# A hybrid decoder layer on one core: paired query loads, merged key and bias loads, six weight splits on VectorE, half of the lead-in fill moved ahead of the value compression

## The chip, the core and the metric

The kernel runs on one core of a Trainium2 chip. The metric is the device time of one launch in microseconds; less is better. The core has a matrix engine (TensorE, PE in the profile; its loads of the stationary operand are shown as PEld), VectorE (DVE), ScalarE (ACT), GpSimd (POOL) and SyncE (SP), which issues all DMAs here.

## The reference

One layer over 1,024 tokens of width 1,024 in float32, cut to what matters:

```python
h = rms_norm(x, attn_norm)
a_conv, q, kc_r, vc_r, ks, vs, kw, vw, g = split(h @ w_in)   # one wide projection
conv_out = swish(layer_norm(causal_depthwise_conv31(u * sigmoid(v))))   # 256 channels
kc, vc = compress(kc_r, ...), compress(vc_r, ...)   # blocks of 32, stride 16: silu(x @ w1) @ w2
# 12 query heads in 4 groups; each group has one key/value head per branch
s_c = softmax(q kc - slope * distance)              # compressed branch; also picks blocks
top = top_k(block_sums(s_c) + forced, 8)            # 8 of 16 blocks of 64 tokens
s_s = softmax(q ks[top] - slope * distance)         # selected branch
s_w = softmax(q kw - slope * distance), last 512 tokens   # window branch
out = g0 * (s_c @ vc) + g1 * (s_s @ vs[top]) + g2 * (s_w @ vw)
x = x + concat(conv_out, out) @ w_out
x = x + (silu(h2 @ w_gate) * (h2 @ w_up)) @ w_down  # h2 = rms_norm(x), hidden width 2816
return rms_norm(x, final_norm)
```

## The kernel before

Every float32 product is three matmuls on a high and a low part: a tile is cast to its high part on ACT, and the low part is the difference, by DVE for activations (`split`) and by POOL for weights (`load_w`: one DMA into one of two `raw` buffers, one ACT cast, and four POOL subtractions of 128x256; three buffers each for high and low part). With `eng` set to another engine, `load_w` makes one subtraction over the whole chunk instead; only the two chunks of the first value projection (`head`) do so before.

The kernel is traced in one order, and a planner places each engine's instructions from that order with simulated times. On the chip every engine then runs its own list strictly in order, and a wait at the head of a list holds all that is behind it. SP's list holds all the DMAs. The kernel has eight PSUM banks in four tags: `s` (2), `t` (3), `o` (1), `z` (2). `turn[1]` names the tags from which `acc_bank` takes the next projection's bank.

The lead-in works on the first 512 tokens (half 0). The `Drive` runs a main line of matmuls, each yielding an estimate of its duration, and steps side jobs when their time has come:

- four conv chunks (`conv_in`, L519), then the two chunks of the key compression's input (`compress_in`, L431), which writes `xh` and `xl` by ACT casts and DVE subtractions; beside it the 62 depthwise taps of half 0 on DVE (`conv_taps`, L537) and POOL's tables (`tables`);
- the window values (`values`, L307, matmuls `vo`);
- the key compression (`compress`, L453: 96 matmuls `h` in four weight chunks), and after each chunk one query projection (`project_d`, L415: 24 matmuls `zo`), in turn by `in_turn`;
- more projections, the value compression's input and the value compression in the same manner, with the stages of the compressed branch (`cmp_stage`, L597) and the tail of the convolution (`conv_tail`, L561) as side jobs. `conv_tail` makes, for each of four token tiles, a transposition `cl`, layer norm on DVE and POOL into `cn`, and after `CONV_LAG` of the drive's time a transposition `cm` of `cn`;
- `compress_v` (L495), which copies the hidden rows to `dup` on DVE and makes the matmuls `vc` from them; then the pools of the lead-in are closed, and the attention's pool `pc` takes their space.

After that 48 matmuls of the fill (`fill_all`: the projections of tokens 512 to 1,023, then output projection and feed-forward) run by themselves, and the rest of the fill is woven into `attention` (L678). Part 0 of the attention has 4 groups of 4 token tiles, part 1 the 4 later tiles of each group. For each tile it does the window branch (br 1) and the selected branch (br 0). `load` (L687), called by the tile's first `scores`, loads keys (in four DMAs) and values once per group, and the tile's queries (in two DMAs, in part 1 a third and three of the bias); queries have two buffers, keys and values one per branch. When the attention is done the second half of the tokens goes through the output projection, and then the feed-forward fills the time to the end.

Of the kernel before, what the change touches and what calls it, by code (L numbers as in the profile page):

```python
# [19 lines left out]
P = 128  # L20
# [59 lines left out]
ACCS2 = "tzz"  # L80
ACCS3 = "z"
PACE_C = 0
CONV_LAG = 5.0
STAGE_GAPS = 5.0, 0.7, 10.0, 0.0
PIECES = 4

# [2 lines left out]
def tile_hymba(ctx: ExitStack, tc, x, attn_norm, w_in, conv_w, conv_b, conv_ln_g, conv_ln_b,  # L89
# [183 lines left out]
    hhi = [quarters(h, 0) for h in range(2)]  # L273
    hlo = [quarters(h, 1) for h in range(2)]

    def win_chunk(c0):
        return load_w([(0, w_in[0, :, c0:c0 + P])], KT, P)


    def value_loads(c0, g0, eng=pool):  # L280
        return [lambda kh=kh: load_w([(0, w_in[0, kh * 512:(kh + 1) * 512, c0:c0 + 256]),
                                      (256, w_in[0, kh * 512:(kh + 1) * 512, C_G + g0:C_G + g0 + 18])], 4, 274, eng)
                for kh in range(2)]
# [30 lines left out]
    for t in range(6):  # L314
        if t < 4:
            if t % 2 == 0:
                x2 = pa.tile([P, 2, DM], F32, tag="xc", name="xt", bufs=2)
            xts.append(x2[:, t % 2, :])
        else:
            xts.append(p2.tile([P, DM], F32, tag="xt", name="xt", bufs=2))  # L320
        sp.dma_start(xts[t], x[0, t * P:(t + 1) * P, :])
        if t == 0:
            grow = a4("grow")
            sp.dma_start(grow, attn_norm[0].partition_broadcast(P))
        if t in (1, 2):
            head.append(value_loads(C_VS, 0, dve)[t - 1]())
        if t == 5:
            first = Feed([lambda c=c: win_chunk(c) for ct in range(2) for c in (CONV + ct * P, ct * P)])
            first.ahead(2)
    for t in range(4):  # L330
        norm_rows(xts[t], xts[t], grow, pa, a4("junk"))
# [346 lines left out]
    def attention(p, bufs, extra, ratio):  # L678
# [8 lines left out]
        def load(st):  # L687
            part, g, i, br = st
            hf = i // 4
            ns = parts[part][-1] + 1  # L690
            if i == parts[part][0]:
                assert not hf or (("kv", g // 2) in done and ("v", g // 2) in done)
                src = (ks_d, kw_d)[br]
                kk = p.tile([P, 2, T], F32R, tag=f"k{br}", name="kt", bufs=bufs["k"])[:, :, :ns * P]
                kf = kk.bitcast(F32)
                sl = src[:, g * 64:(g + 1) * 64, :ns * P]
                sp.dma_start(kf[0:64, 0, :], sl[0])
                sp.dma_start(kf[64:128, 0, :], sl[0])
                sp.dma_start(kf[0:64, 1, :], sl[1])
                if br == 1 or not hf:  # L700
                    sp.dma_start(kf[64:128, 1, :], sl[1])
                else:
                    sp.dma_start(kf[64:80, 1, :], hot_d)
                kt[part, g, br] = kk
                vv = p.tile([P, NT, P], F32R, tag=f"v{br}", name="vt", bufs=bufs["v"])[:, :ns, :]
                sp.dma_start(vv.bitcast(F32), (vs_d, vw_d)[br][:ns * P, g, :].rearrange("(k p) d -> p k d", p=P))
                vt[part, g, br] = vv
            if br == 1:
                cols_i = slice(i * P, (i + 1) * P)
                q2 = p.tile([P, 2, REP, P], F32R, tag="q", name="q2", bufs=bufs["q"])  # L710
                qf = q2.bitcast(F32)
                qs = [q_d[w, g * 192:(g + 1) * 192, cols_i].rearrange("(r d) t -> d r t", d=HD) for w in range(2)]
                sp.dma_start(qf[0:64, 0], qs[0])
                sp.dma_start(qf[64:128, 0], qs[1])
                if hf:
                    sp.dma_start(qf[0:64, 1], qs[0])
                    assert ("bias", g) in done
                    il = i - 4
                    for r in range(REP):
                        sp.dma_start(qf[64:80, 1, r, :], bias_d[g, :, il * P:(il + 1) * P])  # L720
                q2s[g, i] = q2

        def load_pct(st):
            part, g, i, br = st
# [5 lines left out]
        def scores(st, r):  # L730
            part, g, i, br = st
            hf = i // 4
            if r == 0:
                load(st)
            nk = size(st)
            k0 = i + 1 - nk
# [3 lines left out]
            if r == 0:  # L740
                prs[st] = [p.tile([P, REP], F32, tag="l3", name="l3", bufs=26)]
            l3 = prs[st][0]
            q2, kk_ = q2s[g, i], kt[part, g, br]
            if hf:
                pr = p.tile([P, T], F32, tag="pr", name="pr", bufs=bufs["pr"])
            else:
# [5 lines left out]
            for a, e in zip(edges, edges[1:]):  # L752
                s = bank("s", "s")
                sv = s[:, :e - a]
                kk = slice(k0 * P + a, k0 * P + e)
                pe.matmul(sv, q2[:, 0, r, :], kk_[:, 0, kk], start=True, stop=False)  # L756
                if br == 0 and hf:
                    pe.matmul(sv, q2[0:80, 1, r, :], kk_[0:80, 1, kk], start=False, stop=True)  # L758
                else:
                    pe.matmul(sv, q2[:, 0, r, :], kk_[:, 1, kk], start=False, stop=True)  # L760
                dur += 2 * max(0.107, (e - a) / 2400.0)
                mn = p.tile([P, 1], F32, tag="m", name="m", bufs=16)
                t0 = T if br and nk == 5 and a == 0 else T - n + a
                dve.tensor_tensor_reduce(pr[:, a:e], sv, base[:, t0:t0 + e - a], SLOPES[g * REP + r], m,  # L764
                                         ALU.add, ALU.min, mn)
                m = mn
# [59 lines left out]
        for n in range(-1, len(steps)):  # L826
# [7 lines left out]
            asked = max(asked, want)  # L834
            if n < 0:
                load_pct(steps[0])
            elif steps[n][3] and n + 2 < len(steps):
                load_pct(steps[n + 2])
            ts = range(size(steps[n])) if n >= 0 else []
# [41 lines left out]
            yield n  # L881


    def in_turn(main, others, part):
        others = iter(others)
        for n, d in enumerate(main):
            yield d
            if n % part == part - 1:
                yield from next(others, ())
        for o in others:  # L890
            yield from o
# [5 lines left out]
    def mixed_in(a, b):  # L897
        return [ld for pair in itertools.zip_longest(a, b) for ld in pair if ld]

    kvl = kv_loads()  # L900
    first.loads += ([lambda m=m: win_chunk(C_KC + m * P) for m in range(2)] + value_loads(C_VW, 18)
                    + mixed_in(w1_loads(cmp_k_w1), [q_load(m) for m in range(4)]) + [q_load(4), q_load(5)]
                    + [lambda m=m: win_chunk(C_VC + m * P) for m in range(2)] + kvl[:1]
                    + mixed_in(w1_loads(cmp_v_w1), kvl[1:3]) + kvl[3:])
    drive = Drive()
# [6 lines left out]
    drive.run(compress_in(first, 68, xk))  # L912
    drive.run(values(first, 18, vw_d, 0))
    drive.run(in_turn(compress(*xk, first, cmp_k_w2, "s", kk),
                      [project_d(first, q_d, m * P, (0,), True) for m in range(4)], 24))
    turn[1] = ACCS2
    drive.run(project_d(first, q_d, 4 * P, (0,), True))
    compress_k(*kk)
# [9 lines left out]
                      [project_d(first, dst, r, (0,)) for dst, r in ((ks_d, 0), (kw_d, P))], 24))  # L928
    drive.side(stages_in(3))
    drive.run(project_d(first, ks_d, P, (0,)))  # L930
    compress_v(*kv)
    p2_stack.close()
    pa_stack.close()

    pc_stack, pc = open_pool("pc", "right")
    turn[1] = "z"

    def fill_b():
        f1 = Feed([q_load(0), q_load(1)] + value_loads(C_VS, 0) + [q_load(2)] + value_loads(C_VW, 18)
                  + [q_load(m) for m in (3, 4, 5)] + kv_loads() + conv_loads())  # L940
# [267 lines left out]
        yield from conv_tail(1)  # L1208

    fill, slow = fill_all(), conv_rest()  # L1210
    with ExitStack():
        drive.run(itertools.islice(fill, FIRST_B))
        drive.rest()
        weave(attention(pc, BUFS, extra, (RATIO_B, RATIO_C)), fill, (RATIO_B, RATIO_C), slow=slow)
        run(slow)
        pc_stack.close()
        pd_stack, pd = open_pool("pd", "right")
        weave(second(pd), fill, RATIO_D, LEAD_D)
        n0 = early[0]
        early[0] = -1  # L1220
        run(fill)
# [47 lines left out]
```

## Time and profile before

| | |
|---|---|
| median of 3 runs | 1500.84 us (1500.1 to 1503.89) |
| the profiled execution | 1499.39 us |
| its span in the trace | 1497.7 us |
| PE busy | 1447.7 us, 97% |
| mean granted clock of TensorE | 0.991 of full speed |

The span runs from the first to the last instruction of the trace. Busy time is the union of an engine's instructions; matmuls overlap their neighbours, so a busy PE can still run at half of its clock. A number in brackets behind a timeline row is the idle time of that engine just before it, and behind the arrow stands what released it.

### The profile page before, as it was taken

What the parts mean: (1) busy time and instruction counts of PE and PEld (TensorE: products, weight loads), DVE (VectorE), ACT (ScalarE), POOL (GpSimd) and SP (SyncE); (2) the same over time, 40 slices, a digit from 0 to 9 for tenths busy, and PEclk for the clock granted to TensorE, in tenths of its full rate; (3) what the DMA queues carried; (4) which work ended last, traced back from release to release, by engine and by line L of the source; (5) the groups of instructions that cost most, each with busy time, mean ns of one, the idle gap of its engine ahead of it and who ended that gap; (6) DMA issues with size and microseconds to landing.
All of it is one profiled execution on the core that took longest, in us unless ns stands there. A gap on an engine that the chain in (4) does not pass through costs nothing.

```text
span 1497.7 us, 21904 instructions
## 1 busy us (share of the span) xinstructions
PE 1447.7 (97%) x7271; PEld 1214.5 (81%) x7271; DVE 818.4 (55%) x1928; ACT 730.4 (49%) x1477; POOL 839.1 (56%) x1188
## 2 busy tenths in 40 slices
PE   7999989998999999999999999999999999999997
PEld 7788878887878878888888888778788888888885
DVE  6992465778777778687577686222425222222323
ACT  6233577678765676666666655322322222222223
POOL 4666463767766546655655555644533455555554
PEclk9999999999999999999999999999999999999999
DMA  7337477667579334345335223743223323333332
GB/s 231 87 98 199 133 209 235 178 189 188 166 243 242 86 100 121 90 106 130 90 95 141 77 62 93 234 137 95 84 71 108 104 84 99 99 98 98 93 91 84
DMA packets 234222, 193.62 MB, mean 129 GB/s; under 512 B 15881, under 2 KB 204141, under 8 KB 234109
## 3 DMA queue, kind: packets, MB, share of 16 engines
q1 hardware_dynamic: 234108, 192.22, 44.2%
q8 instruction: 58, 0.95, 0.3%
q14 instruction: 56, 0.45, 0.1%
HBM read 158.42 MB, written 33.75 MB: 128 GB/s over the span
## 4 chain that ended last, share of the span: by engine, by line
PE 66%; DVE 4%; DMA 4%; ACT 2%; POOL 2%; issue 1%; SPq 0%; DVEq 0%; POOLq 0%; ACTq 0%
PE gu L1115 30%; PE dn L1135 15%; PE pt L783 4%; PE wo L1055 3%; PE s L756 2%; PE o L801 2%; PE o L800 2%; PE wo L1076 2%; PE s L760 1%; PE s L758 1%; DMA w_raw<-in_w_in_dram 1%; DMA mix<-mix_d 1%; DMA o_raw<-in_w_out_dram 1%; PE cv L145 1%; DVE pl L233 1%
## 5 line engine op out<-in xcount | busy, mean ns | idle before, releaser
L229 POOL TENSOR_TENSOR w_lo<-w_raw,w_hi 128x256 fp32r<-128x256 f32 (+1 forms) x720 | 550.9, 800 | 359.5 <-ACT w_hi L225 346.6
L1115 PE MATMUL gu<-h,w_hi 128*128 128x512 f32 x1408 | 453.4, 396 | 0.0
L225 ACT CAST w_hi<-w_raw 128x1024 fp32r<-128x1024 f32 (+1 forms) x182 | 190.0, 1049 | 364.9 <-PE gu L1115 161.6
L1115 PEld LDWEIGHTS gu<-h,w_hi 128*128 128x128 f32 x1408 | 263.4, 188 | 56.6
L1115 PE MATMUL gu<-h,w_lo 128*128 128x512 f32 x704 | 278.1, 395 | 0.0
L1135 PE MATMUL dn<-w_hi,aw 128*128 128x512 f32 x704 | 234.9, 397 | 2.4 <-DVE af L1122 1.5
L777 POOL TENSOR_SCALAR pr<-pr,l,gates 128x640 f32<-128x640 f32 (+5 forms) x192 | 151.6, 806 | 94.5 <-DVE l L772 86.3
L767 ACT ACTIVATE pr<-pr,m 128x640 f32<-128x640 f32 (+5 forms) x192 | 141.5, 738 | 84.3 <-DVE m L764 77.6
L1140 DVE TENSOR_TENSOR x<-dn,x 128x512 f32<-128x512 f32 x176 | 114.2, 684 | 106.1 <-PE dn L1135 105.5
L1122 DVE TENSOR_TENSOR af<-gu,af 128x512 f32<-128x512 f32 x44 | 30.3, 688 | 240.1 <-PE gu L1115 155.2
L1135 PEld LDWEIGHTS dn<-w_hi,aw 128*128 128x128 f32 x704 | 132.2, 188 | 33.4 <-DVE af L1122 2.2
L233 DVE TENSOR_TENSOR pl<-pt,ph 128x384 fp32r<-128x384 f32 x264 | 139.2, 550 | 36.6 <-ACT ph L233 35.3
L1115 PEld LDWEIGHTS gu<-h,w_lo 128*128 128x128 f32 x704 | 132.3, 188 | 28.6
L233 ACT CAST ph<-pt 128x384 fp32r<-128x384 f32 x264 | 117.5, 478 | 66.6 <-PE pt L783 54.4
L1135 PE MATMUL dn<-w_lo,aw 128*128 128x512 f32 x352 | 138.7, 394 | 0.0
L783 PE MATMUL pt<-ident,pr 128*128 128x128 f32 x792 | 137.0, 273 | 0.6 <-DVE pl L233 0.4
L764 DVE CUSTOM_DVE_ANT_0 pr<-s,base 128x384 f32<-128x384 f32 (+3 forms) x192 | 101.4, 533 | 24.8 <-PE s L760 14.2
L783 PEld LDWEIGHTS pt<-ident,pr 128*128 128x128 f32 x792 | 101.4, 140 | 16.3 <-POOL pr L777 1.7
L145 PE MATMUL zo<-h,w_hi 128*128 128x512 f32 x320 | 108.9, 408 | 4.0 <-ACT af L475 2.3
L756 PE MATMUL s<-kt,q 128*128 128x384 f32 (+3 forms) x288 | 100.3, 351 | 5.0 <-DMA q<-q_d 3.2
L800 PE MATMUL o<-ph,vt 128*128 128x384 f32 x264 | 98.9, 374 | 0.3 <-ACT ph L233 0.3
L801 PE MATMUL o<-pl,vt 128*128 128x384 f32 x264 | 93.2, 353 | 0.5 <-DVE pl L233 0.5
(208 smaller groups left out, 2322.0 us busy)
## 6 DMA issues: line engine op xcount, KB each, us to landing
w_raw<-in_w_gate_up_dram SPq DMA_DIRECT2D x84, 512.0 KB, 3.9
w_raw<-in_w_down_dram SPq DMA_DIRECT2D x42, 512.0 KB, 3.4
w_raw<-in_w_in_dram SPq DMA_DIRECT2D x40, 512.0 KB, 5.0
q<-q_d SPq DMA_DIRECT2D x80, 96.0 KB, 3.4
qc<-q_d SPq DMA_DIRECT2D x32, 192.0 KB, 4.1
pc_d<-pct SPq DMA_DIRECT2D x16, 384.0 KB, 3.4
pct<-pc_d SPq DMA_DIRECT2D x32, 192.0 KB, 3.1
mix_d<-oh SPq DMA_DIRECT2D x64, 96.0 KB, 3.2
```

Of the source, the lines that this page charges most:

```text
L145: lastpe[0] = pe.matmul(*args, **kw)
L225: act.copy(hi[:, :n], raw[:, :n])
L229: eng.tensor_sub(lo[:, q], raw[:, q], hi[:, q].bitcast(F32))
L233: return act.copy(hi, src), dve.tensor_sub(lo, src, hi.bitcast(F32))
L756: pe.matmul(sv, q2[:, 0, r, :], kk_[:, 0, kk], start=True, stop=False)
L767: act.activation(pr[:, :n], pr[:, :n], AF.Exp, bias=m, scale=-1.0, accum_out=l3[:, r:r + 1])
L777: pool.tensor_scalar(x_, x_, l3[:, r2:r2 + 1], gates[:, i, c:c + 1], op0=ALU.mult, op1=ALU.mult)
L783: pe.transpose(pt[:, r * P:(r + 1) * P], prs[st][1 + r][:, kk * P:(kk + 1) * P], ident)
L800: pe.matmul(o[:, :384], v, ph, start=False, stop=False)
L801: pe.matmul(o[:, :384], v, pl, start=False, stop=last)
L1115: pe.matmul(o, w[:, k, :], h2[si][h][k // 4][:, k % 4, :], start=n == 0, stop=n == 3 * KT - 1)
L1135: pe.matmul(o, aws[si][:, a, k, t * P:(t + 1) * P], b[:, 0, ch * 512:(ch + 1) * 512], start=n == 0, stop=n == 5)
```

## The change

- The four conv chunks and the two chunks of the key compression's input have their low parts made by DVE, one subtraction each, instead of four on POOL.
- The first query projection runs whole before the key compression, and the weight chunks are loaded in that order.
- In part 0 one pair of DMAs loads the queries of two token tiles. A group's keys come in two DMAs instead of four (in part 1's selected branch three instead of four). The bias of a tile comes in one DMA with a repeated source instead of three.
- The loads of the first two attention steps stand together ahead of the first scores.
- 24 of the 48 matmuls of the lead-in fill (the first query projection of half 1) stand ahead of `compress_v`, with their bank from tag `t`; the other 24 follow it.
- `CONV_LAG` is 8 instead of 5.

```diff
-CONV_LAG = 5.0
+CONV_LAG = 8.0
...
-    def win_chunk(c0):
-        return load_w([(0, w_in[0, :, c0:c0 + P])], KT, P)
+    def win_chunk(c0, eng=pool):
+        return load_w([(0, w_in[0, :, c0:c0 + P])], KT, P, eng)
...
-            first = Feed([lambda c=c: win_chunk(c) for ct in range(2) for c in (CONV + ct * P, ct * P)])
+            first = Feed([lambda c=c: win_chunk(c, dve) for ct in range(2) for c in (CONV + ct * P, ct * P)])
...
-                sl = src[:, g * 64:(g + 1) * 64, :ns * P]
-                sp.dma_start(kf[0:64, 0, :], sl[0])
-                sp.dma_start(kf[64:128, 0, :], sl[0])
-                sp.dma_start(kf[0:64, 1, :], sl[1])
+                sl = src[:, g * 64:(g + 1) * 64, :ns * P].rearrange("w d t -> d w t")
+                sp.dma_start(kf[0:64], sl)
                 if br == 1 or not hf:
-                    sp.dma_start(kf[64:128, 1, :], sl[1])
+                    sp.dma_start(kf[64:128], sl)
                 else:
+                    sp.dma_start(kf[64:128, 0, :], sl[:, 0, :])
                     sp.dma_start(kf[64:80, 1, :], hot_d)
...
-            if br == 1:
+            if br == 1 and not hf:
+                if i % 2 == 0:
+                    q2 = p.tile([P, REP, 2 * P], F32R, tag="q", name="q2", bufs=bufs["q"])
+                    for w in range(2):
+                        sp.dma_start(q2[w * 64:(w + 1) * 64].bitcast(F32),
+                                     q_d[w, g * 192:(g + 1) * 192, i * P:(i + 2) * P].rearrange("(r d) t -> d r t", d=HD))
+                    for j in range(2):
+                        q2s[g, i + j] = [[q2[:, r, j * P:(j + 1) * P]] * 2 for r in range(REP)]
+            elif br == 1:
...
-                    for r in range(REP):
-                        sp.dma_start(qf[64:80, 1, r, :], bias_d[g, :, il * P:(il + 1) * P])
+                sp.dma_start(qf[64:80, 1], bias_d[g, :, il * P:(il + 1) * P].unsqueeze(1).to_broadcast([16, REP, P]))
...
-            if r == 0:
+            if r == 0 and st not in steps[:2]:
                 load(st)
...
             if n < 0:
                 load_pct(steps[0])
+                load(steps[0])
+                load(steps[1])
...
-    def in_turn(main, others, part):
+    def in_turn(main, others, part, ahead=0):
         others = iter(others)
+        for _ in range(ahead):
+            yield from next(others)
...
-    first.loads += ([lambda m=m: win_chunk(C_KC + m * P) for m in range(2)] + value_loads(C_VW, 18)
-                    + mixed_in(w1_loads(cmp_k_w1), [q_load(m) for m in range(4)]) + [q_load(4), q_load(5)]
+    first.loads += ([lambda m=m: win_chunk(C_KC + m * P, dve) for m in range(2)] + value_loads(C_VW, 18)
+                    + mixed_in([q_load(m) for m in range(4)], w1_loads(cmp_k_w1)) + [q_load(4), q_load(5)]
...
-                      [project_d(first, q_d, m * P, (0,), True) for m in range(4)], 24))
+                      [project_d(first, q_d, m * P, (0,), True) for m in range(4)], 24, 1))
...
-    compress_v(*kv)
-    p2_stack.close()
-    pa_stack.close()
-
-    pc_stack, pc = open_pool("pc", "right")
-    turn[1] = "z"
...
     fill, slow = fill_all(), conv_rest()
+    turn[:] = -1, ACCS2
+    drive.run(itertools.islice(fill, FIRST_B // 2))
+    compress_v(*kv)
+    p2_stack.close()
+    pa_stack.close()
+
+    pc_stack, pc = open_pool("pc", "right")
     with ExitStack():
-        drive.run(itertools.islice(fill, FIRST_B))
+        drive.run(itertools.islice(fill, FIRST_B // 2))
         drive.rest()
+        turn[1] = "z"
```

## Rows read from the trace of the kernel before

**Rows 1.** The page: busy time, share of the span and instructions by engine.
```profile
PE 1447.7 (97%) x7271; PEld 1214.5 (81%) x7271; DVE 818.4 (55%) x1928; ACT 730.4 (49%) x1477; POOL 839.1 (56%) x1188
```

**Rows 2.** PE's timeline, rows with idle time: start, duration, instruction, idle before, releaser.
```profile
42.03 1.09 PE L248 MATMUL tp<-ident,xt 128*128 128x128 f32 x8 [2.29 <-DVE h L233]
...
91.18 0.68 PE L145 MATMUL h<-xh,w_hi 128*128 128x264 f32 x2 [1.74 <-ACT xh L233]
...
205.56 0.41 PE L582 MATMUL cm<-ident,cn 128*128 128x128 f32 x2 [2.67 <-DVE cl L626]
...
208.45 0.79 PE L145 MATMUL zo<-h,w_hi 128*128 128x512 f32 x1 [2.26 <-ACT af L475]
...
242.78 0.30 PE L760 MATMUL s<-kt,q 128*128 128x128 f32 x1 [1.72 <-DMA kt<-ks_d]
...
266.35 0.47 PE L756 MATMUL s<-kt,q 128*128 128x512 f32 x1 [0.81 <-DMA q<-q_d]
...
357.32 0.42 PE L756 MATMUL s<-kt,q 128*128 128x384 f32 x1 [2.39 <-DMA q<-q_d]
...
476.11 0.51 PE L1055 MATMUL wo<-w_hi,mix 128*128 128x512 f32 x1 [1.89 <-DMA mix<-mix_d]
```

**Rows 3.** Windows: length, busy of PE, PEld, DVE, ACT, POOL, clock, DMA, GB/s.
```profile
88.00:92.00 4.00, 2.26 (x16) 2.03 (x14) 3.94 (x8) 1.11 (x3) 0.00 (x0) 0.92 0.61 197
92.00:96.00 4.00, 3.57 (x21) 3.30 (x20) 3.88 (x10) 0.89 (x2) 0.00 (x0) 0.65 0.22 84
204.00:208.00 4.00, 0.63 (x4) 0.42 (x4) 3.10 (x12) 3.95 (x11) 2.34 (x4) 0.93 1.01 242
208.00:212.00 4.00, 3.55 (x8) 2.81 (x9) 3.58 (x9) 3.97 (x8) 4.00 (x6) 0.50 0.43 146
212.00:216.00 4.00, 4.00 (x14) 3.18 (x13) 0.25 (x1) 3.95 (x13) 1.67 (x3) 0.72 0.77 184
356.00:360.00 4.00, 2.68 (x10) 2.20 (x10) 1.30 (x6) 3.55 (x11) 2.42 (x5) 0.70 0.40 129
360.00:364.00 4.00, 4.00 (x21) 3.37 (x21) 3.52 (x11) 2.15 (x7) 3.71 (x8) 0.87 0.38 108
600.00:700.00 100.00, 100.00 (x548) 86.82 (x547) 71.89 (x179) 66.51 (x118) 60.33 (x82) 1.00 0.40 105
```

**Rows 4.** Splits, taps, normalisations by line: ns min/median/max, first and last start.
```profile
L229 POOL TENSOR_TENSOR w_lo<-w_raw,w_hi x720: 715/743/1979, 19.6 to 1475.3; 128x256 fp32r<-128x256 f32 x174, 128x274 fp32r<-128x274 f32 x6
L229 DVE TENSOR_TENSOR w_lo<-w_raw,w_hi x2: 1289/1290/1290, 11.6 to 14.1; 128x1096 fp32r<-128x1096 f32 x2
L553 DVE SCALAR_TENSOR_TENSOR cacc<-y,cols,cacc x62: 705/752/1409, 46.2 to 920.4; 128x512 f32<-128x512 f32 x62
...
L241 DVE SCALAR_TENSOR_TENSOR xt<-xt,rs,grow x8: 1277/1284/7315, 6.6 to 32.8; 128x1024 f32<-128x1024 f32 x8
```

**Rows 5.** Timelines of POOL around 35 us and of DVE at 46 us.
```profile
32.78 2.81 POOL L229 TENSOR_TENSOR w_lo<-w_raw,w_hi 128x256 fp32r<-128x256 f32 x4
...
36.93 3.80 POOL L229 TENSOR_TENSOR w_lo<-w_raw,w_hi 128x256 fp32r<-128x256 f32 x4
...
46.17 5.28 DVE L553 SCALAR_TENSOR_TENSOR cacc<-y,cols,cacc 128x512 f32<-128x512 f32 x5
```

**Rows 6.** Timelines at 205 to 221 us: DVE, ACT and PE.
```profile
204.88 0.54 DVE L576 TENSOR_SCALAR cn<-cl,mv,crs 128x256 f32<-128x256 f32 x1
...
219.90 0.75 DVE L501 CAST dup<-al 128x512 fp32r<-128x512 f32 x2
...
215.04 0.47 ACT L475 ACTIVATE af<-h,bc 128x256 f32<-128x256 f32 x1
...
220.61 0.19 PE L506 MATMUL vc<-w2h,dup 128*128 128x64 f32 x1
```

**Rows 7.** SP's query loads by line; one load on the chain of waits.
```profile
L713 SPq DMA_DIRECT2D q<-q_d x32: 573/598/675, 232.2 to 845.2; - x32
...
351.36 5.87 DMA q<-q_d
```

More of the change, by code (lines that the diff above doesn't have):

```diff
@@ L714, in load @@
                 sp.dma_start(qf[64:128, 0], qs[1])
[L715 to L718, printed above, removed]
-                    for r in range(REP):
-                        sp.dma_start(qf[64:80, 1, r, :], bias_d[g, :, il * P:(il + 1) * P])
-                q2s[g, i] = q2
+                sp.dma_start(qf[0:64, 1], qs[0])
+                assert ("bias", g) in done
+                il = i - 4
+                sp.dma_start(qf[64:80, 1], bias_d[g, :, il * P:(il + 1) * P].unsqueeze(1).to_broadcast([16, REP, P]))
+                q2s[g, i] = [[q2[:, w, r, :] for w in range(2)] for r in range(REP)]
         def load_pct(st):
@@ L742, in scores @@
             l3 = prs[st][0]
-            q2, kk_ = q2s[g, i], kt[part, g, br]
+            q2, kk_ = q2s[g, i][r], kt[part, g, br]
             if hf:
@@ L755, in scores @@
                 kk = slice(k0 * P + a, k0 * P + e)
-                pe.matmul(sv, q2[:, 0, r, :], kk_[:, 0, kk], start=True, stop=False)
+                pe.matmul(sv, q2[0], kk_[:, 0, kk], start=True, stop=False)
                 if br == 0 and hf:
-                    pe.matmul(sv, q2[0:80, 1, r, :], kk_[0:80, 1, kk], start=False, stop=True)
+                    pe.matmul(sv, q2[1][0:80], kk_[0:80, 1, kk], start=False, stop=True)
                 else:
-                    pe.matmul(sv, q2[:, 0, r, :], kk_[:, 1, kk], start=False, stop=True)
+                    pe.matmul(sv, q2[0], kk_[:, 1, kk], start=False, stop=True)
                 dur += 2 * max(0.107, (e - a) / 2400.0)
```

## The prediction, as it was put on record

> **What bounds the kernel now.** I read the page first, then PE's own timeline for its idle places, then windows around those, and last the other engines' timelines beside them. The page says that PE is busy for 1447.7 of 1497.7 us [rows 1], so what an edit can win is PE's idle time, about 50 us (some 15 of it at the two ends), and the time in which PE works at a lowered clock. The change takes no matmul away. PE's timeline shows where the idle time lies: before 560 us, in waits of 0.2 to 2.7 us, eight of which stand in [rows 2]. From 600 to 700 us PE is busy for the whole of the window at full clock [rows 3], and the later stages look the same; nothing done there can help. So each edit is worth what it takes from the waits in the first 360 us.
>
> A wait of two microseconds costs more than itself. After the waits at 91, 205 and 357 us the windows show a granted clock of 0.50 to 0.92, down to the lower of the two levels, 1.2 GHz, at 208 to 212 us [rows 3]. I price this as busy time times what the clock lacks of 1: (0.08 x 2.26) + (0.35 x 3.57) = 1.4 us at 88 to 96; (0.07 x 0.63) + (0.50 x 3.55) + (0.28 x 4.0) = 2.9 at 204 to 216; (0.30 x 2.68) + (0.13 x 4.0) = 1.3 at 356 to 364. The waits at 42, 242 and 266 us have no such price beside them.
>
> **The change part by part.**
>
> *DVE splits.* A chunk's split now takes four POOL instructions of 0.743 us in the median, 3.0 us; on DVE one of 1,096 columns took 1.290 us [rows 4], so 1,024 columns are estimated at 1.21 and six chunks at 7.2 us. They fall between 19 and 60 us, in front of DVE's taps, which leave it hardly any free time (it is busy for 3.94 of 4 us at 88, just before the wait for `xh` [rows 3]). Against this stands what POOL's splits cost DVE. Of eight row normalisations, 1.284 us each in the median, one took 7.315 [rows 4]; it is the last, from 32.84 to 40.16, and ended only in the second of two groups of POOL splits (32.78 and 36.93) [rows 5]. The transposition's wait of 2.29 us at 42.03 follows from it, as the subtraction that frees its bank stood behind it on DVE. The taps at 46 us took 5.28 / 5 = 1.06 us each beside POOL [rows 5], against a median of 0.752 [rows 4]. With the splits off POOL I expect 6.0 us back at the normalisation and about 0.3 on each of 12 taps, 3.6: 9.6 back for 7.2 spent, so the `xl` subtractions behind which the key compression waits end no later. The wait at 42 us goes: 2.3, less 0.5 for a split that stands ahead of a subtraction that PE needs (bounds 0 and two splits, 2.4). I take 1.8.
>
> The Trainium skill has a rule on just this (page "SBUF — State Buffer", section "Who interferes with whom"): of a DVE instruction with two SBUF inputs and a GpSimd instruction that reads SBUF, the second to start waits until the first is finished. By that rule the normalisation would lose one POOL instruction, about 0.7 us; the row shows it losing 6.0, through several of them. Here the row decides, and it makes moving the splits worth more than the rule would.
>
> *Query projection ahead.* PE waits 1.74 us at 91.18 for `xh` [rows 2], and the clock takes 1.4: 3.1 in all. With the change 24 matmuls of 128x512, which at 0.232 us each (24 follow one another in 5.6 us) take 5.6 us, stand between the values and the compression, more than the wait. The chunk order follows the order of use, so the number of loads, casts and splits is the same; each compression chunk is needed 5.6 us later and each projection chunk 3.0 earlier. At the end the last compression chunk has one projection behind it instead of two to hide the way to `kc`; the second was not needed if ACT is free then. Worth 0 to 3.1; I take 2.9.
>
> *CONV_LAG and half of the fill.* The wait of 2.67 us at 205.56 is that of `cm` for `cn`, which DVE finished only at 205.4 [rows 2, 6], and the 2.26 us at 208.45 are the projection behind it, waiting for a bank of tag `t`; with the clock 2.9, so 7.8 us. In the drive's time the second `cm` stands 5 after its `cl`, beside the last compression matmuls; with 8 it comes after the projection that follows, two or three matmuls into the first half of the fill, 5.6 us later on PE. The projection then finds `cm`, `cl` and a bank of the tag free earlier, and both waits go. But something comes back. In the profile `vc` starts at 220.61 without a wait, and that is just when the last DVE copy to `dup` is done (219.90 + 0.75); its chain stood on ACT behind the exponentials of the compressed branch, the second `af` at 215.04 [rows 6]. Without the waits PE is through the projection and the first half of the fill (11.2 us from 202.9) at 214.1, and if the planner puts `vc` right there, PE waits until `dup` is there: between 0 (the chain moves up with PE, or the second half of the fill is put ahead) and 6.5 us, and again a slow clock. The last `cm`, which with the larger lag is left to the end of the drive right behind its `cl`, may cost another 0 to 2.7, the wait of today. I take 3.4 of both, nearer to nothing, since the `cm` work leaves ACT in that stretch: 7.8 - 3.4 = 4.4. On its way the half fill also brings three weight chunks (five DMAs, three casts, twelve POOL splits) ahead of `compress_v`; its copies, subtractions and matmuls are on DVE and PE, and its one ACT cast comes last, so these pass it by. Its bank is one of three of tag `t` for 5.6 us.
>
> *Merged and paired loads.* A query load holds SP for 0.598 us [rows 7]. In part 0 the pairs save 16 of 32, the keys 16 of 32; in part 1 the bias saves 32 issues and the keys 12, off PE's path (600 to 700 us). The pair of tiles 2 and 3 goes into the buffer that the pair of the group before left, instead of waiting for tile 0's last scores of its own group. The load on the chain of waits at 351.36 took 5.87 us to its release of `s` [rows 7] at 357.32; with pairs it can be issued up to a group's tile earlier. That wait with its clock is 2.4 + 1.3 = 3.7; I take 3.3. The 0.81 at 266.35 is an odd tile's, which comes with its pair: 0.6. The 1.72 at 242.78 waits for `ks`, whose load stood behind the queries; hoisted and shorter by two issues it comes several microseconds earlier: 1.4. Each could save nothing if the larger transfer lands later by as much.
>
> *Sum.* 1.8 + 2.9 + 4.4 + 3.3 + 0.6 + 1.4 = 14.4 us. Since the planner makes the order anew, I count one new wait like that at 476.11, 1.89 us [rows 2] and 1.3 for the clock: -3. That leaves 11.4. The profiled execution, 1499.39 us, becomes 1488.0; it was 1.45 below the median, so the median becomes 1489.
>
> **The rivals.**
>
> 1. *The waits move on.* `vc` and the last `cm` get back all of it (6.5 + 2.7), and the reorder another such wait. Then 14.4 becomes 14.4 - 5.8 - 6 = 2.6: 1498, within the noise. For it speaks that `vc` has no slack today; against it, that the fill's other half and the values are independent work that may be put ahead. Chance 0.20.
>
> 2. *All of it is kept.* The six places give 2.3 + 3.1 + 7.8 + 1.7 + 0.8 + 3.7 = 19.4 us and no new wait comes: 1481. For it speaks that PE has independent work at every one of them; against it, the many in-order lists. Chance 0.12.
>
> 3. *Later landing at the group changes: slower.* A key load of one transfer twice as long has to land whole before the first scores of a group; keys have a single buffer per branch, so the load can't start earlier. If this shows as a wait like the one at 357 us, it costs 3.7 us at each of the 16 group loads. Three of them take back what I forecast; from five on (18.5) the kernel is slower by over 0.3%: 1489 + 18.5 = 1507. Against it speaks that the bytes are the same, that SP is done two issues (1.2 us) sooner, and that today only one group load shows a wait, the 1.72. Chance 0.10.
>
> **How the numbers follow.** The forecast, 1489, has 0.58. Runs of this kernel lie within 0.25% of each other, so I call 0.3%, 4.5 us, the bound of what can be told: faster means under 1496.3. The forecast and rival 2 are faster, 0.70; rival 1 is the same, 0.20; rival 3 slower, 0.10. The range runs from rival 2's time to just beyond rival 1's, 1480 to 1501, and leaves out rival 3 and little else.
>
> **What would show it.** Right: no idle above 1 us before the late transpositions near 40 us; the normalisation at 1.3 us; no wait for `xh` at the first `h`; no wait for `cn` at 200 to 210 us and a clock of 1.00 there; no wait of `s` for a query DMA near 350 us. Wrong: a wait before `vc` of over 3 us, a slow clock at 212 to 230 us, a new wait at a group's first scores, or DVE's taps that end later than now, with the first `h` waiting still.

## The result, and the profile after

The changed kernel takes 1514.7 us in the median of 4 runs (1511.62 to 1516.43), before takes 1502.37 on the same chip (1500.1 to 1504.54). The ratio is 1.008, with a 95% interval of 1.0055 to 1.0105: it is slower, by 12 us, where 1489 was forecast. The profiled execution took 1514.14 us, its span 1512.4.

PE has 7271 matmuls as before. The page's line of busy times answers to [rows 1]: POOL has lost the six chunks' splits, PE is busy 7.7 us longer and idle 7.0 us longer.

```profile
PE 1455.4 (96%) x7271; PEld 1217.2 (80%) x7271; DVE 817.8 (54%) x1934; ACT 724.8 (48%) x1473; POOL 821.5 (54%) x1164
```

PE's timeline after, rows with idle time, to be held against [rows 2]:

```profile
104.99 0.52 PE L145 MATMUL h<-xh,w_hi 128*128 128x264 f32 x2 [1.39 <-ACT w_hi L225]
106.11 0.81 PE L145 MATMUL h<-xh,w_lo 128*128 128x264 f32 x2 [0.60 <-POOL w_lo L229]
139.05 0.39 PE L491 MATMUL kc<-ah,w2h 128*128 128x256 f32 x1 [3.56 <-ACT ah L233]
206.18 0.50 PE L145 MATMUL zo<-h,w_hi 128*128 128x512 f32 x1 [0.92 <-ACT cf L585]
270.35 0.52 PE L145 MATMUL vo<-w_hi,h 128*128 128x274 f32 x2 [2.06 <-ACT w_hi L225]
352.56 0.80 PE L145 MATMUL zo<-h,w_hi 128*128 128x512 f32 x1 [2.88 <-ACT w_hi L225]
495.05 0.79 PE L1058 MATMUL wo<-w_hi,mix 128*128 128x512 f32 x1 [2.77 <-DMA mix<-mix_d]
1025.83 1.20 PE L1079 MATMUL wo<-o_hi,mix 128*128 128x512 f32 x4 [1.55 <-ACT o_hi L1005]
1058.16 2.82 PE L248 MATMUL tp<-ident,rows 128*128 128x128 f32 x12 [3.01 <-DVE rows L241]
```

The six places that the forecast named are clean: no wait at 42 and at 91, 0.92 us instead of 4.93 near 205, no `s` that waits for a load. In their stead stand the weights at 105, `kc` at 139, weights again at 270 and 352, and two waits behind 1,000 us, in stages that no edit touches. The windows of [rows 3], after, show the same: full clock and a busy PE at 88 to 96 and at 208 to 216, where before had 0.92, 0.65, 0.50 and 0.72.

```profile
88.00:92.00 4.00, 4.00 (x27) 3.69 (x26) 3.87 (x9) 1.02 (x2) 0.00 (x0) 1.00 0.64 220
92.00:96.00 4.00, 4.00 (x27) 3.61 (x26) 4.00 (x5) 3.01 (x4) 3.52 (x4) 1.00 0.18 66
204.00:208.00 4.00, 3.08 (x20) 2.64 (x19) 3.33 (x13) 3.92 (x8) 3.25 (x6) 1.00 1.00 264
208.00:212.00 4.00, 4.00 (x21) 3.20 (x19) 3.43 (x7) 2.19 (x4) 4.00 (x6) 1.00 0.84 237
212.00:216.00 4.00, 4.00 (x21) 3.02 (x18) 1.52 (x5) 3.43 (x13) 1.15 (x2) 1.00 0.48 131
356.00:360.00 4.00, 4.00 (x16) 3.31 (x15) 1.90 (x7) 2.41 (x12) 0.74 (x2) 0.70 0.27 102
```

**Where the time went.** Waits alone don't tell it, since two orders can't be compared by the clock on the wall. So I give each matmul of both traces one fixed price, the usual spacing of its shape in before, and ask when each kernel has done the same amount of this work. The table below names an amount by the time at which before had done it, and gives how much later (+) the other kernel had. (To be ahead or behind is always meant against before.) The changed kernel is 2.1 us ahead at 81 us, 2.5 behind at 181, 3.0 ahead again at 225, 6.5 behind at 384, 5.3 behind at 950, and 15.0 behind from 1,107 to the end. Three losses, then: 4.6 us around the key compression, 9.5 in the first part of the attention, 9.7 in the second output projection; and two gains, 2.1 and 5.5, which are the DVE splits and the waits at 205. The 9.5 is the least firm of them: the difference swings with each wait of either kernel, and at 480 us the changed kernel is only 1.7 behind.

The last loss is plain in the windows too. The second set's output projection and norm lie between 960 and 1,080 us; PE starts 166 + 174 + 186 = 526 matmuls there before, and 161 + 163 + 163 = 487 after. From 950 to 1,110 us PE is idle for 2.0 us before and for 7.8 after. Windows of before, then of the changed kernel:

```profile
960.00:1000.00 40.00, 38.83 (x166) 31.05 (x167) 11.31 (x18) 7.19 (x11) 18.52 (x26) 1.00 0.37 113
1000.00:1040.00 40.00, 40.00 (x174) 32.43 (x173) 7.22 (x10) 10.41 (x15) 21.90 (x31) 1.00 0.47 157
1040.00:1080.00 40.00, 39.18 (x186) 31.58 (x185) 19.73 (x30) 16.59 (x26) 20.62 (x29) 1.00 0.26 79
```
```profile
960.00:1000.00 40.00, 38.22 (x161) 29.40 (x160) 9.34 (x14) 8.73 (x12) 15.29 (x21) 1.00 0.38 112
1000.00:1040.00 40.00, 38.20 (x163) 29.88 (x162) 6.93 (x10) 8.45 (x13) 22.37 (x32) 1.00 0.45 151
1040.00:1080.00 40.00, 35.96 (x163) 28.80 (x162) 19.33 (x30) 14.43 (x24) 16.79 (x24) 0.96 0.24 73
```

One piece of it can be followed by hand. DVE's normalisation needs the row of norm weights, which SP loads in 0.58 us of issue. Before, SP issued it at 1044.21 and DVE normalised at 1047.92. After, SP's list has a weight load ahead of it, and that one waited for a buffer until POOL's split was over (1047.23 + 3.33 us); so the row was issued at 1051.02 and DVE went on at 1056.82. SP and POOL, then DVE, of the changed kernel:

```profile
1047.23 3.33 POOL L229 TENSOR_TENSOR w_lo<-w_raw,w_hi 128x256 fp32r<-128x256 f32 x4
...
1050.59 0.38 SPq L224 DMA_DIRECT2D w_raw<-in_w_gate_up_dram  x1
1051.02 0.58 SPq L1087 DMA_DIRECT2D rows<-in_ffn_norm_dram  x1
...
1056.82 3.68 DVE L241 SCALAR_TENSOR_TENSOR rows<-x,rs,rows 128x1024 f32<-128x1024 f32 x3 [4.07 <-DMA rows<-in_ffn_norm_dram]
```

The same of before, with the transpositions on PE behind it:

```profile
1044.21 0.33 SPq L1084 DMA_DIRECT2D rows<-in_ffn_norm_dram  x1
...
1047.92 1.28 DVE L241 SCALAR_TENSOR_TENSOR rows<-x,rs,rows 128x1024 f32<-128x1024 f32 x1 [1.32 <-DMA rows<-in_ffn_norm_dram]
...
1049.26 1.09 PE L248 MATMUL tp<-ident,rows 128*128 128x128 f32 x8 [0.67 <-DVE rows L241]
```

So the row explains a part only: DVE stood 4.07 us for it instead of 1.32, and PE's transpositions behind it 3.01 instead of 0.67.

Two theories follow. "Edit": the lag, the half fill and the projection ahead lose by what they do. "Order": small edits make the planner lay out the attention and all that is woven into it anew, and that order is worse than the one of before, whatever the edit was.

### The profile page after: what moved, and what is told of

It is laid out like the page before. It is cut to its first block, busy times and chain, and to the rows that moved or that the text cites. A ratio compares the mean times of both kernels' runs of the same rounds, so it can differ in the third digit from the quotient of the medians.

```text
span 1512.4 us, 21784 instructions
## 1 busy us (share of the span) xinstructions
PE 1455.4 (96%) x7271; PEld 1217.2 (80%) x7271; DVE 817.8 (54%) x1934; ACT 724.8 (48%) x1473; POOL 821.5 (54%) x1164
## 4 chain that ended last, share of the span: by engine, by line
PE 68%; DMA 10%; DVE 9%; POOL 5%; ACT 4%; issue 3%; SPq 0%; DVEq 0%; ACTq 0%; POOLq 0%
PE gu L1118 30%; PE dn L1138 15%; PE pt L789 5%; DMA w_raw<-in_w_in_dram 4%; PE zo L145 3%; POOL w_lo L229 3%; PE wo L1058 3%; PE o L807 2%; PE o L806 2%; PE s L762 2%; DMA o_raw<-in_w_out_dram 2%; DVE cacc L553 2%; PE zc L145 1%; DMA mix<-mix_d 1%; POOL o_lo L1008 1%
## 5 line engine op out<-in xcount | busy, mean ns | idle before, releaser
L229 POOL TENSOR_TENSOR w_lo<-w_raw,w_hi 128x256 fp32r<-128x256 f32 (+1 forms) x696 | 530.5, 795 | 361.5 <-ACT w_hi L225 348.7
L789 PEld LDWEIGHTS pt<-ident,pr 128*128 128x128 f32 x792 | 102.8, 141 | 18.7 <-POOL pr L783 1.9
```

The source lines that it names most:

```text
L229: eng.tensor_sub(lo[:, q], raw[:, q], hi[:, q].bitcast(F32))
L789: pe.transpose(pt[:, r * P:(r + 1) * P], prs[st][1 + r][:, kk * P:(kk + 1) * P], ident)
```

## The experiments

All 18 runs, beside before (1501.4 to 1502.4 in their calls). The six middle columns are the table described above, from one profiled execution each. The last counts the feed-forward matmuls that PE starts ahead of the second output projection (before: 1107). Kernels that do the same as before in the first 80 us lie 0.6 to 3.9 us behind it there, so differences of that size in these columns are scatter between executions. The profiled execution of before, with which all are compared, was some 2 us below its medians, that of `changed_lag_5` some 10 us above its own and that of `changed_lag_12` 5; so the column at 1107 is not the difference of the medians.

| kernel | median us | ratio, 95% | at 81 | 181 | 225 | 384 | 950 | 1107 | ffn ahead |
|---|---|---|---|---|---|---|---|---|---|
| changed | 1514.7 | 1.0055–1.0105 | -2.1 | +2.5 | -3.0 | +6.5 | +5.3 | +15.0 | 1100 |
| dve_only | 1498.2 | 0.9952–0.9982 | -2.7 | -3.0 | -1.9 | -5.0 | -5.1 | -5.9 | 1107 |
| loads_only | 1497.3 | 0.9952–0.9985 | +3.6 | +3.3 | +5.7 | +4.6 | -1.4 | -2.8 | 1107 |
| ahead_only | 1504.3 | 0.9994–1.0031 | +3.3 | +3.5 | +5.1 | +0.6 | +0.8 | +0.2 | 1107 |
| half_only | 1526.2 | 1.0130–1.0174 | +3.9 | +1.9 | -3.7 | +4.4 | +15.5 | +27.2 | 1080 |
| lag_only | 1519.1 | 1.0099–1.0145 | +0.6 | +0.7 | -4.5 | -0.3 | +18.7 | +22.3 | 1029 |
| half_fill_only | 1530.2 | 1.0169–1.0220 | +1.4 | +0.6 | +2.5 | +10.2 | +23.8 | +34.1 | 1078 |
| without_half | 1500.5 | 0.9964–1.0001 | -2.5 | +4.0 | +7.9 | +6.7 | +4.0 | +2.9 | 1107 |
| splits_and_loads | 1495.5 | 0.9948–0.9979 | -2.8 | -3.1 | +0.9 | -1.0 | -3.7 | -5.8 | 1107 |
| gap_plus_one | 1519.2 | 1.0075–1.0137 | +2.7 | +0.8 | 0.0 | +6.1 | +8.5 | +18.0 | 1078 |
| lag_5_5 | 1523.9 | 1.0113–1.0165 | +3.6 | +1.2 | -0.9 | +3.2 | +23.3 | +25.9 | 1025 |
| fill_51 | 1521.7 | 1.0101–1.0153 | +2.2 | +1.0 | +6.3 | +8.5 | +18.1 | +25.4 | 1078 |
| changed_lag_5 | 1510.3 | 1.0030–1.0080 | -2.7 | +3.9 | +4.9 | +15.0 | +19.2 | +21.2 | 1107 |
| splits_loads_lag_8 | 1508.8 | 1.0023–1.0055 | -2.5 | -1.4 | -6.8 | -1.6 | +11.0 | +11.0 | 1107 |
| splits_loads_gap | 1510.5 | 1.0032–1.0075 | -2.2 | -2.6 | -2.5 | +5.9 | +11.3 | +10.9 | 1107 |
| two_projections_behind | 1508.0 | 1.0024–1.0066 | -2.6 | -3.0 | -5.5 | +0.2 | +3.3 | +10.7 | 1078 |
| changed_lag_12_no_ahead | 1495.2 | 0.9926–0.9968 | -2.2 | -2.0 | -9.2 | -5.4 | -3.7 | -3.6 | 1107 |
| changed_lag_12 | 1500.3 | 0.9971–1.0006 | -2.2 | +2.8 | -5.5 | +4.0 | +7.2 | +6.3 | 1107 |
| changed_lag_9_two_behind | 1493.4 | 0.9930–0.9956 | -2.7 | -2.2 | -8.7 | -4.9 | -6.6 | -5.9 | 1107 |

### Each part by itself

Four kernels, each before with one part of the diff: `win_chunk(c, dve)`; `in_turn(..., 24, 1)` with its load order; the half fill with the lag of 8; the loads.

> Only the six low parts by VectorE; all else as before. Theory A (each edit loses or wins at its own place): the wait at 42 us goes and nothing else changes much, 2 to 4 us faster, so 1498 to 1501 beside a before of 1502, with the gain all ahead of 100 us. Theory B (the planner's new order costs time in stages that the edit does not touch): the gain ahead of 100 us is the same 2 to 4, but the time to the second set's feed-forward moves by another 5 to 10 us, either way, behind 200 us.

> Only the first query projection ahead of the key compression, with its load order. Theory A: the loss of 9.6 us between 95 and 155 us in the changed kernel is this edit's: the weight feed runs dry near 105 us, and the last compression chunk has only one projection behind it, so kc waits 3 to 4 us; against the wait of 1.74 us for xh that goes, 3 to 7 us slower, 1505 to 1509. Theory B: the same places move by under 3 us net, and the difference arises behind 200 us, either way. Prediction's own step: 2.9 us faster, 1499.

> Only the lag of 8 and half of the lead-in fill ahead of the value compression. Theory A: the wait of 2.67 and 2.26 us near 205 us go (5 to 8 us), and 10 us come back between 220 and 290 us because the value compression ends later and the attention starts later; net 2 to 5 us slower, 1504 to 1507. Theory B: 4 us faster at 290 us, as predicted, and what is lost is lost at other places behind it. Prediction's own step: 4.4 us faster, 1498.

> Only the loads: queries in pairs, merged key and bias loads, the first two steps' loads ahead of the first scores. Theory A: no wait of scores for a load is left, 3 to 5 us faster up to 450 us and nothing behind, 1497 to 1499. Theory B: 3 to 5 us faster up to 450 us, and 5 to 10 us given or taken between 450 and 1080 us, above all where the second token half's norm row is loaded near 1050 us. Rival 3 of the prediction (larger loads land later): new waits of scores for keys at the 16 group loads, 3.7 us each, 1515 or more.

The splits win 3.7 us and the loads 4.6, each against before's 1501.9, and neither loses anything later; rival 3's waits at the group loads don't come. The projection ahead, alone, is not told from no change; the wait of `kc` that theory "edit" had put on it isn't in its trace, where PE comes to `kc` at 140.81 and `ah` is ready. Compared from the end backwards, PE's list of matmuls is that of before from 64 us on with the splits, from 140 on with the projection ahead, and from 950 on with the loads. Between 237 and 950 us the loads have another list than before too, and lose nothing by it: so not every redrawn order is a worse one. The half fill with its lag loses 24 us, far more than theory "edit" had put on it, and only 4.4 of them show by 384 us: the rest comes later in the attention and behind 950, far from the edit.

### The half taken apart, and the rest put together

```diff
-CONV_LAG = 5.0
+CONV_LAG = 8.0
```

> Only the lag of 8 instead of 5 for the convolution's tail. With lag and half fill together the kernel takes 1526 us (24 more than before). Theory A (moving the half fill costs it): this run keeps the gain at 205 us alone, 4 to 8 us faster, 1494 to 1498. Theory B (the longer lag costs it, since the tail's last tiles then run into the start of the attention): 15 to 24 us slower, 1517 to 1526. Theory C (neither by itself, the planner's redrawn order scatters): within 5 us of before with losses at other places than in the run of both.

> Only the half of the lead-in fill ahead of the value compression; the lag stays at 5. Theory A: about 31 matmuls of the fill have run before the first scores that before were cover for the first attention steps, the attention runs at its old pace with less fill beside it, and the fill is some 45 matmuls behind at 490 us: 15 to 25 us slower, 1517 to 1527. Theory B: no loss behind 250 us, within 4 us of before, 1498 to 1506. Theory C: between them, 1505 to 1515.

> The changed kernel without the half fill and with the old lag: VectorE splits, query projection ahead, and the loads remain. If the four parts add up: -3.7 (splits) +2.4 (projection ahead) -4.6 (loads) = 6 us under before, 1496, so 18 us under the changed kernel. If the half fill is what loses and its loss does not depend on the rest, the same. Theory C (scatter of the order): anything from 1490 to 1512, not the sum. It also shows whether the loss between 95 and 155 us stays (theory: it does, at 7 to 10 us, since it needs the splits' earlier start and the projection ahead together) and whether the loss at 1050 us goes.

> Only the VectorE splits and the loads. If the parts add up: -3.7 - 4.6 = 8 us under before, 1493 to 1494, the best of all. Theory C: anything from 1490 to 1505. If the query projection ahead is what loses between 95 and 155 us, this run has no loss there and starts the value compression 5 to 8 us ahead of before.

One constant costs 17 us, the other half of the pair 28, and both together 24: they don't add, so these are not two fixed costs, each of its own edit. `lag_only` has lost nothing by 384 us, and its tail of the convolution ends with the last `cm` at 231.6, ahead of the first scores of the attention (233.1): the tail doesn't run into the attention, as one expectation had it. What the rest does is clearer. Splits and loads add up nearly (6.3 of 8.3 us), and putting the projection ahead costs 5.0 us on top (1500.5 against 1495.5), all of it by 181 us: +4.0 against -3.1.

### Edits that do no work

```diff
-STAGE_GAPS = 5.0, 0.7, 10.0, 0.0
+STAGE_GAPS = 5.0, 0.7, 11.0, 0.0
...
-CONV_LAG = 5.0
+CONV_LAG = 5.5
...
-FIRST_B = 48
+FIRST_B = 51
```

Each is a kernel of its own, before with one constant changed and no work added or taken away (a null edit); the fourth is the changed kernel with `CONV_LAG = 5.0`.

> The kernel before with one of the compressed branch's stage gaps in the lead-in at 11 instead of 10 us of the drive's time. Nothing of the work or of its dependencies changes, and the stage has a dozen microseconds to spare; the planner's order of TensorE differs from the 800th row to the end of the attention. Theory 'order' (any small edit of the lead-in redraws the attention's order, and a redrawn order is worse than the one of before by 10 to 30 us): 1512 to 1530. Theory 'edit' (the lag and the half fill lose by what they do, a longer tail and a later value compression): 1502, within 4 us of before.

> The kernel before with the lag at 5.5 instead of 5. A lag of 8 by itself took 1519. Theory 'order': redrawn as much as with 8, 1510 to 1525, whatever the size of the step. Theory 'edit': a sixth of the step of 3, so a sixth of the loss of 17, or none, 1502 to 1505.

> The kernel before with 51 instead of 48 matmuls of the fill ahead of the attention, 0.7 us of TensorE's work that only changes places. Theory 'order': 1510 to 1530. Theory 'edit': 1502, within 4 us of before.

> The changed kernel with the lag at 5 again; the half fill and the rest stay. Theory 'edit': the loss of the half fill stays, and that of the lag goes, so between 1501 (all but the half fill) and 1515. Theory 'order': another draw, with no relation to the sum of the parts: the half fill alone took 1530, and this may take 1505 to 1530.

All three null edits lose what theory "order" said, 18, 22 and 20 us, and theory "edit" had none of it. A lag of 5.5 loses more than one of 8. `changed_lag_5`, 1510.3, fell where both theories allowed it and decides nothing. In `gap_plus_one` the windows read as in the changed kernel (167 + 154 + 165 = 486 matmuls):

```profile
960.00:1000.00 40.00, 38.72 (x167) 30.93 (x166) 9.96 (x15) 7.84 (x13) 18.71 (x26) 1.00 0.42 132
1000.00:1040.00 40.00, 36.97 (x154) 29.70 (x153) 7.07 (x11) 8.64 (x12) 20.86 (x29) 0.96 0.45 151
1040.00:1080.00 40.00, 36.98 (x165) 29.21 (x164) 20.90 (x30) 15.24 (x25) 17.86 (x22) 0.96 0.18 56
```

### The two stretches told apart

Where the count of the last column is 1107, PE's list of matmuls from 950 us to the end is that of before, one for one. The next four were chosen by their lists: three keep that stretch.

> VectorE splits, the loads, and the lag of 8; neither the half fill nor the projection ahead. In the order of this kernel the feed-forward has 1107 matmuls ahead of the second output projection, as in before, and the stretch behind that is in the order of before; with lag 8 alone it was 1029. Theory 'order' in its narrower form (what loses is the order in which fill and attention come out, not the lag): nothing is lost behind 950 us, the waits near 205 us go (5 to 7 us), and the redrawn first part of the attention costs 0 to 10: 1489 to 1500 beside 1495.5 for splits and loads. Theory 'edit' (the lag itself costs 17): 1508 to 1515.

> VectorE splits and the loads, with the stage gap of 11 instead of 10, which took before to 1519. Here the order behind 950 us stays that of before, and only the attention's is redrawn. If the two stretches of loss are separate: the one behind 950 us (8 to 10 us) is absent, and the one between 200 and 480 us (6 to 9 us in the run on before) is there, 1500 to 1506. If any redraw of the attention costs its 18 us: 1513. If the loads make the attention insensitive to its order: 1493 to 1498.

> VectorE splits, the loads and the projection ahead, but with two projections instead of one between the last chunk of the key compression and the matmuls kc. Theory: the 3.3 us wait of kc for ah goes, and the matmuls behind it run 5 to 6 us earlier than in the run without the half fill (about 1.5 us behind splits and loads alone at 150 us, since the weight feed still lags); PE's waits near 105 us for weights, 2.8 us in sum, stay. Rival: ah comes late because of the casts on ACT whatever stands behind the chunk, and kc waits 2 us or more still. The order of the attention is redrawn, with 1078 feed-forward matmuls ahead of the second output projection: for the whole time, 'order' expects 1505 to 1520, and without an effect of the order it would be 1494 to 1497.

> The changed kernel without the projection ahead and with the lag at 12: splits, loads, half fill. The order behind 950 us is that of before. If the half fill has no cost of its own: the waits at 205 us are gone and nothing is lost behind 950, 1488 to 1498. If the half fill costs by itself between 215 and 290 us, where the value compression is drawn out and the attention starts later (12 us in the run with lag 5): 1500 to 1510, with the loss in that stretch.

The stretches are separate. All three with 1107 lose nothing behind 950 us (at most 0.1). But the redrawn attention alone costs 13 and 15 us in the first two, more than I had expected, and the time of `splits_loads_lag_8` fell where "edit" had put it. Yet a lag doesn't lose by its size: with a lag of 12, and the half fill too, the kernel takes 1495.2.

`two_projections_behind` moves `compress_k` behind one more projection. The wait for `ah` is gone, though its `af` still stands behind a cast and a table load and comes only 0.8 us sooner than in the changed kernel (137.33 against 138.08); its rows on ACT, and `kc` on PE:

```profile
134.97 1.05 ACT L225 CAST w_hi<-w_raw 128x1024 fp32r<-128x1024 f32 x1 [3.23 <-POOL xl L436]
136.03 1.28 ACT L475 ACT_TABLE_LOAD   x1
137.33 0.48 ACT L475 ACTIVATE af<-h,bc 128x256 f32<-128x256 f32 x1
...
140.11 0.28 PE L491 MATMUL kc<-ah,w2h 128*128 128x256 f32 x1
```

At 181 us it is level with splits and loads alone (-3.0 against -3.1), so the 7 us that the projection ahead costs by then in `without_half` (+4.0) go when `kc` has its second projection as cover. They are more than the wait of 3.31 us for `ah` in that kernel, in part because PE's granted clock from 130 to 145 us was 0.79 there and is 1.00 here. The window, first of `without_half`, then of `two_projections_behind`:

```profile
130.00:145.00 15.00, 11.50 (x42) 9.10 (x43) 3.48 (x9) 7.23 (x12) 9.64 (x17) 0.79 0.59 174
```
```profile
130.00:145.00 15.00, 15.00 (x69) 12.28 (x68) 3.48 (x7) 8.78 (x14) 9.60 (x16) 1.00 0.60 177
```

The kernel's whole time, 1508.0, is what "order" had expected: its count is 1078, and it loses 7.4 us between 950 and 1,107.

### The changed kernel with another draw

A draw stands here for one of the orders that the planner may come to.

```diff
-CONV_LAG = 8.0
+CONV_LAG = 12.0
```

The second kernel has a lag of 9 and `compress_k` behind the projection that followed it.

> The changed kernel with one number changed, the lag at 12 instead of 8. Its order from the attention to the end is that of the run without the projection ahead (1495.2), which kept the order of before behind 950 us. If the parts now add: 1495.2 plus the 5.0 that the projection ahead cost beside splits and loads, 1500, 15 us below the changed kernel. If the projection ahead or the half fill undo it together: 1505 to 1515. If a lag acts by its size: slower than the changed kernel, 1520 or more.

> The changed kernel with two projections between the last chunk of the key compression and kc, and the lag at 9; its order behind 950 us is that of before. If the kc wait is what the projection ahead costs and the order decides the rest: no wait of kc, 1488 to 1497. If the redrawn attention loses as in splits and loads with the gap: 1500 to 1508, with the loss between 200 and 480 us.

With all five edits kept and one constant changed, the changed kernel takes 1500.3, as the sum had it, 14 us less. The second takes 1493.4, 0.57% under before (interval 0.44% to 0.70%), and is the fastest measured, though its interval and that of splits and loads alone overlap.

The table shows which of the two losses the lag of 12 takes away: the one behind 950 us (-0.9 instead of +9.7). Between 225 and 384 us this kernel loses 9.5 like the changed one, in one execution of each. So the loss behind 950 is shown to be the order's. The one in the attention stays, and the table's columns at 225 and 384 say this of it: the seven kernels with the half fill lose 3.8 to 10.1 us there, the seven other redrawn ones 2.2 to 8.4, and the five with the attention's order of before or of the loads gain 1.1 to 4.5. A redrawn attention loses there with the half fill or without it; whether the half fill adds a share of its own is not told apart.

## Why the prediction was wrong

**The step that failed first** is the last term of the sum: "since the planner makes the order anew, I count one new wait like that at 476.11 ... -3". That term was mis-sized: it is the largest of all. Null edits cost 18 to 22 us. The half fill and the lag, in the order that they got, cost 14.2 (1514.7 against 1500.5), and another order of the same edits takes 14.4 less (1500.3). In the changed kernel's own trace the two stretches lose 9.5 and 9.7; that the first of them is the order's alone, and none of it the half fill's, is not shown. With it falls the sentence that from 600 us on "nothing done there can help": no edit helps there, but another order of the second output projection costs time. (The kernel before also had a few short waits behind 560 us, the longest 1.31 us at 812.) Over the 18 runs and the changed kernel, the eleven with 1107 matmuls ahead move by -2.1 to +2.0 us between 950 and 1,107, the eight others lose 2.6 to 11.7. PE's idle time from 950 to 1,110 us says the same without any price: 0.6 to 3.2 us in the eleven, 4.6 to 9.3 in the eight.

**The step that failed by itself** is the projection ahead: "the second was not needed if ACT is free then", worth 0 to 3.1, with no loss in the bounds. ACT was not free. It takes its list in order, and `af` stood behind the cast of a weight chunk that was still on its way, and behind a table load. ACT, changed kernel:

```profile
135.73 1.04 ACT L225 CAST w_hi<-w_raw 128x1024 fp32r<-128x1024 f32 x1 [4.77 <-DMA w_raw<-in_w_in_dram]
136.79 1.28 ACT L475 ACT_TABLE_LOAD   x1
138.08 0.47 ACT L475 ACTIVATE af<-h,bc 128x256 f32<-128x256 f32 x1
138.59 0.41 ACT L233 CAST ah<-af 128x256 fp32r<-128x256 f32 x1
```

So `kc` waited 3.56 us. The kernel before had a cast and a table load ahead of this `af` too, and there the second projection hid them, so that `kc` started without a wait. ACT and PE of before:

```profile
132.92 1.05 ACT L225 CAST w_hi<-w_raw 128x1024 fp32r<-128x1024 f32 x1 [1.75 <-DMA w_raw<-in_w_in_dram]
133.99 1.28 ACT L475 ACT_TABLE_LOAD   x1
135.28 0.47 ACT L475 ACTIVATE af<-h,bc 128x256 f32<-128x256 f32 x1
...
137.47 0.28 PE L491 MATMUL kc<-ah,w2h 128*128 128x256 f32 x1
```

And the gain of 2.9 was not there either: PE without its wait at 91 ran into the weights at 105 (1.39 and 0.60). "The number of loads, casts and splits is the same" was right and not enough, since PE came to them sooner.

**What held.** The DVE splits: the wait at 42 is gone, 1.8 forecast, 3.7 measured alone. The row that paid for it (after, by line) answers to [rows 4]: the slowest normalisation took 2.061 us instead of 7.315, and a split on DVE 1.248 in the median of eight, two of them over 1,096 columns; 1.21 had been estimated for 1,024.

```profile
L229 DVE TENSOR_TENSOR w_lo<-w_raw,w_hi x8: 1210/1248/1577, 11.6 to 49.8; 128x1024 fp32r<-128x1024 f32 x6, 128x1096 fp32r<-128x1096 f32 x2
...
L241 DVE SCALAR_TENSOR_TENSOR xt<-xt,rs,grow x8: 1278/1284/2061, 6.6 to 37.6; 128x1024 f32<-128x1024 f32 x8
```

The Trainium skill (page "SBUF — State Buffer", section "Who interferes with whom") would have had the normalisation wait for one GpSimd instruction. With POOL's splits beside it the normalisation of the kernel before lost 6.0 us, so here the measurement differs from the page. Without them, in the changed kernel, it lost 0.78 us, within the one POOL instruction of 1.72 us that was running when it began.

The loads: 3.3 + 0.6 + 1.4 = 5.3 forecast, 4.6 measured, and in the changed kernel's trace every wait of `s` for a load is gone. The waits at 205: the forecast of 7.8 with 3.4 coming back is what the changed trace shows by 225 us (5.5 net), but it was lost again in the attention. Even in the good draw it buys nothing: `changed_lag_12_no_ahead` is 10 us ahead of splits and loads at 225 us (-9.2 against +0.9) and 2 behind at 1,107; by the medians they are equal (1495.2 and 1495.5).

Of the rivals, the first had the direction (the waits move on) and too small a price, 5.8 + 6. The one that ended slower, larger loads that land later, did not come. What made the kernel slower is the reorder, which the forecast counted as one wait and the first rival as two.

**What stays open.** Why a list of before runs with fewer stops than its redrawn forms is shown only in places, as at the row of norm weights. Late weights (`w_hi` at 270 and 352 in the changed kernel) are frequent in the redrawn attention, and late `mix` stands in before too; no run forced one list onto another kernel. That before's list is a good one among many is shown by three null edits and the two with a gap or a lag on splits and loads; how many lists are as good is not known.

## What to carry to other kernels

Where a planner lays out a kernel anew for each edit, measure a null edit first: its scatter (here 18 to 22 us) is the size below which an edit's own gain of 3 to 8 us can't be read from the total, unless the order has stayed. Read each edit from the time at which equal work is done, in the stretch that it touches, and draw another order before dropping it. An edit that brings PE forward needs its feed brought forward too: ask what the weights, casts and table loads behind it on in-order lists will do, and keep two pieces of independent work where two were.

## What the runs showed of the hardware

The wait at 42 us came out differently in kernels whose PE does the same up to there: 2.29 us in before and in `lag_only`, 4.03 in `loads_only` and `gap_plus_one`, 5.28 in `half_only`, with the slowest normalisation beside POOL's splits at 7.31 us in each. No run shows why. And one cast of 1.04 us on ACT that waited 4.77 us for its data, with a table load of 1.28 us behind it, stopped PE for 3.56 us.
